# A hybrid streaming-encoder block on one core: x turned from token rows on TensorE, a plain first unit, and units, weights and gate writes in another order

## The chip, the core and the metric

The kernel runs on one core of a Trainium2 chip. A core has five engines with their own instruction queues: TensorE (PE, matrix products and transposes; its weight loads are shown apart as PEld), VectorE (DVE), ScalarE (ACT), GpSimd (POOL) and SyncE (SP, which here only issues DMAs). Sixteen DMA engines move data between the chip's memory and the core. The metric is the device time of one execution in microseconds (us); less is better.

## The reference

One layer: x and mem are normed and projected, three token mixers run side by side, each is projected back and gated, their sum is projected and added to x, and a gated feed-forward follows. There are 1024 tokens, 1024 channels and 256 memory tokens.

```python
h = _rmsnorm(x, norm_mix_g[l])
z = h @ w_in[l]
(hq, hf, hi, hg, fq, fk, fv, ff, mq, gate_logits) = jnp.split(z, pts, axis=-1)
y_a = _hgrn2_mixer(hq, hf, hi, hg, lower_bounds[l], hgrn_norm_g[l])      # 4 heads x 128, chunks
y_b = _fox_mixer(fq, fk, fv, ff, fox_f_bias[l], fox_q_norm_g[l], fox_k_norm_g[l])  # 8 heads x 64
mem_kv = _rmsnorm(mem, norm_mem_g[l]) @ mem_kv_w[l]
y_c = _memory_mixer(mq, mem_kv, mem_q_norm_g[l], mem_k_norm_g[l])        # 4 heads x 128
gates = jax.nn.sigmoid(gate_logits).reshape(B, T, N_BRANCH, D_MODEL)
merged = gates[:, :, 0] * (y_a @ w_br_hgrn[l]) + gates[:, :, 1] * (y_b @ w_br_fox[l]) + ...
x = x + merged @ w_out[l]
h2 = _rmsnorm(x, norm_ffn_g[l])
x = x + _conv_glu_ffn(h2, ffn_w_up[l], ffn_conv_w[l], ffn_conv_b[l], ffn_w_down[l])
```

`ff` (8 columns) gives the logits of the forget factors of the attention: log-sigmoid of them, summed along the tokens, is the bias of the attention's logits.

## The kernel before

**Products.** An fp32 product is made of three fp32r products (`mm3`): each operand is split into a high part (`h`, a rounding cast on ScalarE, line 115) and a low part (`l`, a subtraction on VectorE, line 123), and h·h, h·l and l·h are summed in PSUM (lines 109 to 111). The input projection is done in units by a Strassen-Winograd scheme on a 2 x 2 split of x (channel halves c, token halves n): seven products of 48 instructions instead of eight. The operands on the side of x are seven *families*: B11, B21, B22 are blocks of the normed x, T1, T2, T3, T4 are differences of them. Each has a high and a low tile.

**Stages.** (1) *Opening*: memory keys and values (`kv_chunk`, eight weight pieces wkv), the square sums of x, which is loaded with channels on partitions (`xT`, tiles xk), its rstd (by products with `ones`, spread over the partitions by `spread`), the forget logits as plain fp32 products of wff and x (line 315), and the first families. (2) *Five token-major units* (`tm_unit`), whose products are 256 columns wide: hi (values of HGRN), mq (memory queries), fox queries and keys of pairs 0 and 1, of pairs 2 and 3, and fv. A unit's outputs are normed per head (`head_norm`), turned by transposes and written to DRAM (kqd, vhd, hid, mqd). The steps of the memory attention (`mem_attn`) are queued in a list and woven into the units, up to STAGE_STEPS = 3 behind each product. (3) *Eighteen channel-major units* (`cm_unit`), 512 columns wide: six for HGRN (f, q, g), twelve for the gates, and then the branch projections. They are a generator, `fill`, that is woven as TensorE's filling work into (4) *the forgetting attention* (`fox_attn`, 8 heads; its steps have a higher priority by AHEAD = 300, and FOX_FILL says how many steps of fill go beside each head) and (5) *the HGRN mix* (`hgrn_mix`, 4 heads, HGRN_FILL steps beside each). The rest of the fill runs behind it, then (6) the *channel mixer* with `w_out`, `w_up`, `w_dn`.

**Order.** Instructions go to an engine's queue in the order that a scheduler gives at build time; each engine runs its queue in order. A DMA belongs to the queue of the engine that issues it, and stands there with its waits. A tile has a fixed number of buffers (`bufs`): whoever writes it next waits until its readers are done. A pool (`xp`, `rp`, `mp`, `ur`, `pfam`) holds space on a side of the on-chip memory until its release; the pool behind it starts where its space comes free.

**Names.** pp, lg, tr and po are the four kinds of PSUM banks. `w_tm` and `w_cm` are the weights of the two kinds of units, loaded into `raw` and `ur`; `ur` has 3 buffers of 512 KB here. `mskf` is the causal mask, `nf` the forget bias of a head, kh/qa/kl its keys and queries. uo is an output of a channel-major unit, written to `gd` (gates) or `hgd` (HGRN) and loaded from there later.

## Time and profile before

| | before |
|---|---|
| median of 3 runs | 1781.06 us (1780.62 to 1783.25) |
| profiled execution | 1782.18 us |
| its span | 1780.4 us |
| mean granted clock of TensorE | 0.982 |
| busy, share of the span | PE 96%, PEld 81%, DVE 70%, ACT 47%, POOL 27% |
| DMA | 272 MB, mean 153 GB/s |
| instructions in the profile | 25032 |

The profile counts an instruction as busy from its start to its end; since TensorE overlaps neighbours, its busy time is not its work, and the distance from start to start is the better price. `PEclk` is the TensorE clock that was granted, as a part of full speed. The table of stages gives the busy time of each engine in a stretch of the span with the number of its instructions in brackets. A row of a wait reads: who waited, for which engine's tile and line, total us, number, longest. A row in order of time reads: start, duration, engine, line, operation, out<-in, shape, count, and in brackets the idle time before it and who ended it.

### The profile page before, as it was taken

The numbers are of one execution on the slowest core, as the hardware profiler recorded it, in microseconds if no ns is written. First come the engines' busy times: TensorE is split into PE (matmuls) and PEld (weight loads), VectorE is DVE, ScalarE is ACT, GpSimd is POOL, SyncE is SP. The second block draws the span as 40 slices with busy tenths as digits, with TensorE's granted clock in tenths as the row PEclk, the third lists the DMA queues.
The fourth block names the chain that finished last, engine by engine and source line by source line (L and its number), as shares of the span: only waits on it lengthen the run. The fifth ranks groups of instructions, "written<-read, shape, count | busy, mean of one in ns | idle before, by whom it ended". The sixth has DMA issues, their size and how long they took to land.

```text
span 1780.4 us, 25032 instructions
## 1 busy us (share of the span) xinstructions
PE 1709.9 (96%) x8960; PEld 1443.3 (81%) x8960; DVE 1249.2 (70%) x2239; ACT 838.9 (47%) x1430; POOL 482.6 (27%) x496
## 2 busy tenths in 40 slices
PE   7799999989999999998999899999999999999999
PEld 5589999868888888877888788788888888878887
DVE  6967665447766676599799665787877877775654
ACT  6455555436565656566443333543433444433332
POOL 1644554335544434254223000111111111100000
PEclk9899999999999999999999999999999999999999
DMA  7034352484544443424543452455545444394772
GB/s 289 25 120 160 131 188 86 148 220 135 144 143 137 138 143 97 168 89 164 168 140 121 136 184 83 142 158 178 154 132 160 125 124 135 135 379 146 231 276 84
DMA packets 114398, 272.03 MB, mean 153 GB/s; under 512 B 11960, under 2 KB 29112, under 8 KB 113632
## 3 DMA queue, kind: packets, MB, share of 16 engines
q1 hardware_dynamic: 97088, 215.36, 36.8%
q0 software_dynamic: 14880, 52.96, 10.6%
q10 hardware_dynamic: 2304, 2.10, 0.3%
q8 instruction: 71, 1.16, 0.3%
q14 instruction: 55, 0.45, 0.1%
HBM read 202.93 MB, written 90.51 MB: 165 GB/s over the span
## 4 chain that ended last, share of the span: by engine, by line
PE 80%; DMA 6%; DVE 5%; issue 3%; POOL 3%; ACT 2%; SPq 0%; DVEq 0%; ACTq 0%; POOLq 0%
PE pp L109 17%; PE pp L111 17%; PE pp L110 17%; PE lg L111 4%; PE lg L109 4%; PE lg L110 4%; PE tr L109 2%; PE tr L110 2%; PE tr L111 2%; PE lg L1023 1%; DMA kh<-kqd 1%; POOL ws L424 1%; PE po L932 1%; PE lg L890 1%; PE lg L891 1%
## 5 line engine op out<-in xcount | busy, mean ns | idle before, releaser
L1282 POOL DMA_DIRECT2D rw<-in_w_up x44 | 24.3, 557 | 343.7 <-DVE wl L123 176.7
L115 ACT CAST wh<-s 128x512 fp32r<-128x512 f32 x85 | 51.9, 619 | 125.8 <-PE pp L110 65.3
L115 ACT CAST dwh<-wr 128x1024 fp32r<-128x1024 f32 (+1 forms) x42 | 41.1, 980 | 123.2 <-PE tr L110 42.0
L109 PE MATMUL pp<-yh,bwh 128*128 128x512 f32 x192 | 78.1, 412 | 5.1 <-ACT bwh L115 1.8
L115 ACT CAST wh<-rw 128x512 fp32r<-128x512 f32 x65 | 40.0, 619 | 86.1 <-PE pp L110 46.9
L1004 POOL TENSOR_TENSOR X<-X,kt 128x256 f32<-128x256 f32 x48 | 50.1, 1049 | 107.4 <-ACT X L1003 96.3
L110 PE MATMUL pp<-yl,bwh 128*128 128x512 f32 x192 | 78.1, 407 | 0.3 <-DVE yl L123 0.3
L111 PE MATMUL pp<-yh,bwl 128*128 128x512 f32 x192 | 77.8, 407 | 0.0
L123 DVE TENSOR_TENSOR dwl<-wr,dwh 128x1024 fp32r<-128x1024 f32 (+1 forms) x42 | 47.5, 1132 | 40.8 <-ACT dwh L115 40.4
L906 ACT ACTIVATE pt<-pt,st 128x128 f32<-128x128 f32 (+3 forms) x64 | 49.8, 778 | 51.0 <-DVE st L905 25.0
L123 DVE TENSOR_TENSOR ul<-us,uh 128x512 fp32r<-128x512 f32 x72 | 54.7, 763 | 25.7 <-ACT uh L115 24.8
L908 POOL TENSOR_SCALAR pt<-pt,st 128x128 f32<-128x128 f32 (+3 forms) x64 | 52.3, 819 | 61.0 <-DVE st L907 49.3
L677 POOL TENSOR_TENSOR us<-ur 128x512 f32<-128x512 f32 x36 | 51.8, 1438 | 56.6 <-DMA ur<-in_w_cm 40.0
L115 ACT CAST uh<-us 128x512 fp32r<-128x512 f32 x72 | 44.1, 617 | 36.7 <-PE pp L110 21.6
L123 DVE TENSOR_TENSOR wl<-s,wh 128x512 fp32r<-128x512 f32 x85 | 58.0, 682 | 4.9 <-ACT wh L115 4.9
L885 POOL TENSOR_TENSOR nfm<-nf,mskf 128x128 f32<-128x128 f32 x64 | 33.5, 523 | 91.6 <-DVE st L896 50.4
L123 DVE TENSOR_TENSOR wl<-rw,wh 128x512 fp32r<-128x512 f32 x65 | 43.7, 685 | 19.0 <-PE pp L111 15.1
L896 DVE CUSTOM_DVE_ANT_0 pt<-lg,nf 128x512 f32<-128x512 f32 (+2 forms) x80 | 41.3, 525 | 21.9 <-PE lg L891 11.1
L677 POOL TENSOR_TENSOR us<-us,ur 128x512 f32<-128x512 f32 x36 | 46.9, 1303 | 27.8 <-DVE ul L123 25.1
L110 PE MATMUL pp<-dbl,dwh 128*128 128x512 f32 x132 | 51.8, 392 | 1.5 <-DVE dbl L123 1.5
L123 DVE TENSOR_TENSOR pl<-tr,ph 128x512 fp32r<-128x512 f32 (+1 forms) x80 | 49.4, 629 | 4.5 <-ACT ph L115 4.2
L111 PE MATMUL pp<-dbh,dwl 128*128 128x512 f32 x132 | 51.9, 393 | 0.0
(580 smaller groups left out, 6312.0 us busy)
## 6 DMA issues: line engine op xcount, KB each, us to landing
rw<-in_w_up POOLq DMA_DIRECT2D x44, 512.0 KB, 4.7
ur<-in_w_cm SPq DMA_DIRECT2D x36, 512.0 KB, 3.7
sd<-in_w_dn POOLq DMA_DIRECT2D x30, 512.0 KB, 5.9
br<-yd SPq DMA_DIRECT2D x30, 512.0 KB, 5.0
gd<-uo SPq DMA_DIRECT2D x48, 256.0 KB, 2.1
gt<-gd SPq DMA_DIRECT2D x48, 256.0 KB, 3.0
yd<-fc SPq DMA_DIRECT2D x44, 256.0 KB, 2.2
raw<-in_w_tm SPq DMA_DIRECT2D x20, 512.0 KB, 5.5
```

What stands on the lines that cost most here:

```text
L109: PE.matmul(ps, lh, rh, start=first, stop=False, skip_group_check=more)
L110: PE.matmul(ps, lh, rl, start=False, stop=False, skip_group_check=more)
L111: PE.matmul(ps, ll, rh, start=False, stop=last, skip_group_check=more)
L115: S.copy(out, in_)
L123: return (sub or V).tensor_sub(l, src, h.bitcast(F32))
L677: G.tensor_add(t, a, b)
L885: G.tensor_tensor(nfm, nf[:, tsl], mskf, ALU.add)
L896: V.tensor_tensor_reduce(out=pt[:, s0 + lo:s0 + hi], in0=ps[:, lo:hi], in1=bias, op0=ALU.add, op1=ALU.max, scale=1.0, scalar=-3e38, accum_ ...
L906: S.activation(pt[:, :ns], pt[:, :ns], AF.Exp, bias=st[:, 2:3], accum_out=st[:, 3:4])
L908: G.tensor_scalar(pt[:, :ns], pt[:, :ns], st[:, 3:4], 0.0, ALU.mult, ALU.add)
L1004: G.tensor_mul(Xk, Xk, Kv[:, :, 0, :])
L1282: late["raw"] = G.dma_start(raw[:, 2 * i:2 * i + 2, :], src[:, 2 * i:2 * i + 2, :])
```

## The change

**x.** In the mixer, x comes no longer with channels on partitions but as eight tiles of 128 token rows (`x_rows`), placed in the space of the families T2 and T1, which are made later. ScalarE squares a row tile and sums along it in the same instruction (`row_square`); VectorE scales each row by its rstd (`row_norm`); TensorE turns the rows into the channel layout by 64 transposes (`turn_x`, four to a block of 128 x 512), and ScalarE copies each block out of PSUM with the channel's gain into a quarter `xq`. The square sums by products with `ones`, the spreading of rstd and `normed` are gone from the opening. `xT` is still loaded for the residual in the channel mixer.

**Units.** The first token-major unit is now mq, and it is a plain product (`first_unit`): eight products of 48 instructions with the families B11, B21, B12 (in T4's space) and B22. The other families are made beside it (`second_half`, `differences`, `third`, `last`), with subtractions on VectorE where GpSimd had them. The order of units is mq, hi, fox pairs 0 and 1, fv, fox pairs 2 and 3. All steps of the memory attention are queued in unit hi, two behind each product; the memory's keys and values are finished in the first unit and written by SP.

**Forget logits.** They are computed in unit two from the families B11, B21, B22 and T3, with weights split into a high and a low part that stand side by side in 40 columns: 16 products of 40 x 512 and 16 of 8 x 512 in fp32r.

**Others.** The first weight pieces of unit one and the x rows are loaded between the kv pieces. `head_norm` squares into the PSUM bank instead of a tile. A channel-major unit loads four pieces of 256 KB into 5 buffers. The 48 gate writes are issued by ScalarE instead of SP. HGRN_FILL is 32, 30, 28, 22 instead of 24, 24, 24, 20. The attention, the HGRN mix and the channel mixer keep their instructions; line numbers move by 15 to 50.

```diff
-HGRN_FILL = [24, 24, 24, 20]
+HGRN_FILL = [32, 30, 28, 22]
-STAGE_STEPS = 3
+STAGE_STEPS = 2
...
+    xr = [fam_tile(f, p, (P, 2, T), F32) for f in ("T2", "T1") for p in "hl"]
...
+    xq = [[xp.tile([P, 4, HB], F32, tag=f"x{c}{n}", name=f"x{c}{n}") for n in range(2)] for c in range(2)]
...
-        if q > 1:
-            load_x(q - 2)
-    SP.dma_start(ones, mats[:, P:2 * P])
+        load_x(q - 1)
+    SP.dma_start(ident, mats[:, 0:P])
+    load_x(3)
+    load_kv(4)
+    load_kv(5)
+    load_x(4)
+    tm_load(0, (0,))
+    load_x(5)
+    load_kv(6)
+    load_x(6)
+    tm_load(0, (1,))
+    load_x(7)
+    load_kv(7)
+    tm_load(0, (2, 3))
...
-    def forget_logits():
-        for k in range(KC):
-            for n in range(2):
-                PE.matmul(pairs[1][n][:8, :], wff[:, k, :], xk[k][:, n * HB:(n + 1) * HB], start=k == 0, stop=k == KC - 1)
...
+    def row_square(tb):
+        S.activation(ws_tile("sq"), x_row(tb), AF.Square, accum_out=rowsum[:, tb:tb + 1])
+
+    def row_norm(n):
+        ns = slice(4 * n, 4 * n + 4)
+        rstd_small(rt[:, ns], rowsum[:, ns], D)
+        for tb in range(4 * n, 4 * n + 4):
+            V.tensor_scalar(x_row(tb), x_row(tb), rt[:, tb:tb + 1], None, ALU.mult)
+
+    def quarter(c, n, k):
+        return xq[c][n][:, k, :]
+
+    def turn_x(c, n, k):
+        ps = ps_tr()
+        for b in range(4):
+            PE.transpose(ps[:, b * P:(b + 1) * P], x_row(4 * n + b)[:, (4 * c + k) * P:(4 * c + k + 1) * P], ident)
+        S.activation(quarter(c, n, k), ps, AF.Copy, scale=col(C_GX + 4 * c + k))
...
-    with tc.issue_after(spreads.ins):
-        forget_logits()
...
-    def normed(c, n, k, eng=V):
-        q = quarter(c, n, k)
-        if eng is V:
-            V.scalar_tensor_tensor(out=q, in0=q, scalar=col(C_GX + k + 4 * c), in1=rx[:, n * HB:(n + 1) * HB],
-                                   op0=ALU.mult, op1=ALU.mult)
-        else:
-            S.activation(q, q, AF.Copy, scale=col(C_GX + k + 4 * c))
-            G.tensor_mul(q, q, rx[:, n * HB:(n + 1) * HB])
-        return q
...
+    def first_half(c):
+        for k in range(4):
+            turn_x(c, 0, k)
+            family_block("B21" if c else "B11", k, quarter(c, 0, k))
+
+    for q in range(8):
+        if q < 4:
+            mem_chunk(2 * q)
+            mem_chunk(2 * q + 1)
+        kv_chunk(q)
+        if 0 < q < 4:
+            row_square(q - 1)
+        elif q == 4:
+            row_square(3)
+            row_norm(0)
+            for m in range(2):
+                S.copy(mkt[:, m, :], pairs[0][m])
+        elif q == 5:
+            first_half(0)
+            row_square(4)
+            row_square(5)
+        elif q == 6:
+            first_half(1)
+            row_square(6)
+    row_square(7)
+    row_norm(1)
...
+    def second_half():
+        fam["B12"] = [fam_tile("T4", p) for p in "hl"]
+        new_family("B22")
+        for c, name in enumerate(("B12", "B22")):
+            for k in range(4):
+                turn_x(c, 1, k)
+                family_block(name, k, quarter(c, 1, k))
+
+    def differences():
+        new_family("T2")
+        for k in range(4):
+            t2 = xp.tile([P, HB], F32, tag="tt", name="tt", bufs=2)
+            V.tensor_sub(quarter(0, 0, k), quarter(0, 0, k), quarter(0, 1, k))
+            V.scalar_tensor_tensor(out=t2, in0=quarter(0, 0, k), scalar=-1.0, in1=quarter(1, 1, k),
+                                   op0=ALU.mult, op1=ALU.subtract)
+            family_block("T2", k, t2)
+            V.scalar_tensor_tensor(out=quarter(1, 0, k), in0=t2, scalar=-1.0, in1=quarter(1, 0, k),
+                                   op0=ALU.mult, op1=ALU.subtract)
+        new_family("T1")
+        for k in range(4):
+            family_block("T1", k, quarter(0, 0, k))
...
+    def third():
         for k in range(4):
             q = quarter(0, 1, k)
-            G.tensor_sub(q, quarter(1, 1, k), q)
+            V.tensor_sub(q, quarter(1, 1, k), q)
             family_block("T3", k, q)
-        for k in range(4):
-            family_block("B22", k, quarter(1, 1, k), G)
...
+    def first_unit(put):
+
+        banks = [pairs[i] for i in (0, 1, 2, 0)]
+        ops = [tm_operand(raws[0, i]) for i in range(3)]
+        h, l = ws_tile("w4h", F32R), ws_tile("w4l", F32R)
+        split(S, h, l, raws[0, 3])
+        ops.append([t.rearrange("p (k c) -> p k c", k=4) for t in (h, l)])
+        for i, (c, n) in enumerate(((0, 0), (1, 0), (0, 1), (1, 1))):
+            for j, name in enumerate(("B12", "B22") if n else ("B11", "B21")):
+                tm_product(banks[i], ops[2 * c + j], name, j == 0)
+                if j:
+                    put(c, n, tm_out(0, banks[i], None), banks[i])
+                if i == 3:
+                    tm_load(1, range(2 * j, 2 * j + 2))
+                yield
...
+    def forget_logits():
+        wf = mem["mp"].tile([P, 2, KC, 40], F32R, tag="wf", name="wf")
+        wff, sm = (mem["mp"].tile([P, KC, 8], F32, tag=t, name=t) for t in ("wff", "sm"))
+        SP.dma_start(wff, w_ff)
+        V.memset(wf.bitcast(F32), 0.0)
+        V.tensor_add(sm[:, 0:4, :], wff[:, 0:4, :], wff[:, 4:8, :])
+        V.tensor_scalar(sm[:, 4:8, :], wff[:, 0:4, :], -1.0, None, ALU.mult)
+        for n, w in enumerate((wff, sm)):
+            split(S, wf[:, n, :, 0:8], wf[:, n, :, 32:40], w)
+        ff = ko_tile("ff", F32).rearrange("p a b -> p (a b)")
+        for n, names in enumerate((("B11", "B21"), ("B22", "T3"))):
+            ps = ps_tr()
+            sl = slice(n * HB, (n + 1) * HB)
+            for c, name in enumerate(names):
+                h, l = fam[name]
+                for k in range(4):
+                    w = wf[:, n, 4 * c + k, :]
+                    PE.matmul(ps[:40, :], w, h[:, k, :], start=c + k == 0, stop=False, skip_group_check=True)
+                    PE.matmul(ps[:8, :], w[:, 0:8], l[:, k, :], start=False, stop=c * k == 3, skip_group_check=True)
+            S.copy(ff[:8, sl], ps[32:40, :])
+            V.tensor_add(ff[:8, sl], ff[:8, sl], ps[:8, :])
+        SP.dma_start(ffd, ff[:8, :])
...
-            sq = mp.tile([P, HB], F32, tag="fsq", name="fsq").rearrange("p (c d) -> p c d", c=2 * nh)
+            sq = bank[b].rearrange("p (c d) -> p c d", c=2 * nh)
...
+    stage(0, put_mq, (None, second_half, memory, differences, None, third))
+    small_consts()
+    stage(1, put_hi, (last, mem_steps, forget_logits, forget_row))
     stage(2, put_fqk(0))
-    stage(3, put_fqk(1))
+    stage(3, put_fv)
...
+    stage(4, put_fqk(1))
...
-            SP.dma_start(gd[i, n], t)
+            S.dma_start(gd[i, n], t)
...
-        for i in range(2):
-            t = ur.tile([P, 2, HB], F32, tag="ur", name="ur", bufs=3)
+        for i in range(4):
+            t = ur.tile([P, HB], F32, tag="ur", name="ur", bufs=5)
             SP.dma_start(t, w_cm[u, i])
-            raw += [t[:, 0, :], t[:, 1, :]]
```

On TensorE, before the change, the end of the opening: the last forget products (L315, with wff the forget weights), eight products that spread rstd (L301, `ident` as an operand), and the first products of unit hi with family B11.

```order
L315 MATMUL pp<-xk_113,wff 8x512
L315 MATMUL po<-xk_113,wff 8x512
L315 MATMUL pp<-xk_114,wff 8x512
L315 MATMUL po<-xk_114,wff 8x512
L301 MATMUL tr<-ident,B22h 128x128 x8
L109 MATMUL pp<-wh,B11h 128x256
L110 MATMUL pp<-wl,B11h 128x256
L111 MATMUL pp<-wh,B11l 128x256
```

TensorE at the same place after the change; the x rows stand in the space named T1h and T1l, L337 is `turn_x`, and T4h and T4l are the memory tokens' space, as before.

```order
L109 MATMUL lg<-wh,T4h 128x512
L110 MATMUL lg<-wl,T4h 128x512
L111 MATMUL lg<-wh,T4l 128x512
L337 MATMUL tr<-ident,T1h 128x128 x2
L337 MATMUL tr<-ident,T1l 128x128 x2
L110 MATMUL pp<-wl,B11h 128x256
L111 MATMUL pp<-wh,B11l 128x256
L109 MATMUL pp<-wh,B11h 128x256
```

The products of the memory's values (out lg) now stand right ahead of the last turns and of unit one, and no forget products and no spreading stand between.

On SP, before the change, the start of the channel-major units and of the attention: the last writes of fv (vhd), the first weight loads (ur, 512 KB each), the writes of HGRN's inputs (hgd), and the first loads of head 0 (kh).

```order
L642 DMA vhd_74<-vo 128x1024
L735 DMA ur<-in_w_cm 128x1024
L722 DMA hgd_78<-uo 128x512
L642 DMA vhd_75<-vo 128x1024
L735 DMA ur<-in_w_cm 128x1024
L865 DMA kh_3572<-kqd_70 64x1024
L866 DMA kh_3572<-kqd_70 64x1024
```

SP at the same place after the change, with the writes of the last fox unit (kqd) where those of fv stood.

```order
L622 DMA kqd_72<-ko 256x1x512 x2
L784 DMA ur<-in_w_cm 128x512 x3
L622 DMA kqd_73<-ko 256x1x512 x2
L771 DMA hgd_78<-uo 128x512
L914 DMA kh_3661<-kqd_70 64x1024
L915 DMA kh_3661<-kqd_70 64x1024
```

The loads of head 0 now follow the first hgd write directly, behind smaller weight loads; the mask is issued behind 15 loads of the first two heads in both orders.

On TensorE, before the change, the end of the HGRN mix: state products (L1056, L1054), the transposes of the last output (L1075), and the branch products of the fill (yh, yl and bwh, bwl).

```order
L111 MATMUL pp<-yh_9620,bwl 128x512
L1056 MATMUL po<-St,qe 128x128
L1054 MATMUL po<-hi_9452,A 128x128
L1056 MATMUL po<-St,qe 128x128
L1075 MATMUL tr<-ident,o_9744 128x128 x4
L109 MATMUL pp<-yh_9622,bwh 128x512 x3
L110 MATMUL pp<-yl_9623,bwh 128x512
```

TensorE there after the change, first the last state products (L1105, L1103) and then the first transposes (L1124); 24 products of the fill stand between the two pieces.

```order
L1105 MATMUL po<-St,qe 128x128
L1103 MATMUL po<-hi_10026,A 128x128
L1105 MATMUL po<-St,qe 128x128
L110 MATMUL pp<-yl_9540,bwh 128x512
L111 MATMUL pp<-yh_9539,bwl 128x512
```

```order
L109 MATMUL pp<-yh_9539,bwh 128x512
L1124 MATMUL tr<-ident,o_10284 128x128
L110 MATMUL pp<-yl_9540,bwh 128x512
L111 MATMUL pp<-yh_9539,bwl 128x512
L109 MATMUL pp<-yh_9541,bwh 128x512
L1124 MATMUL tr<-ident,o_10284 128x128 x3
```

Products of the fill now stand ahead of the last transposes and between them.

More of the change, by code (lines that the diff above doesn't have):

```diff
@@ L342, in tile_block @@
-    for n in range(2):
-        spreads = spread(rx, rt, (n,))
-    with tc.issue_after(spreads.ins):
-        forget_logits()
-    def quarter(c, n, k):
-        return xk[k + 4 * c][:, n * HB:(n + 1) * HB]
     def new_family(name):
```

243 lines of the change are left out of this document (98 added, 145 removed).

## The prediction

> **What bounds the kernel now.** I read the table of stages first: for each stretch the busy time of every engine, the granted clock of TensorE and the share and rate of the DMA engines. The stretches are the opening up to the first product of a token-major unit, that unit, the other four units, the start of the forgetting attention, its body, the HGRN mix, its tail, the rest of the fill, and the channel mixer.
>
> ```profile
> core 0: us, PE busy (x) PEld busy (x) DVE busy (x) ACT busy (x) POOL busy (x), PEclk, DMA share, GB/s
> 0.00:57.50 57.50, 46.32 (x168) 27.12 (x169) 40.12 (x67) 33.59 (x48) 12.03 (x14) 0.97 0.61 223
> 57.50:119.50 62.00, 48.58 (x339) 46.81 (x338) 52.33 (x52) 31.22 (x51) 44.80 (x26) 0.83 0.29 95
> 119.50:331.70 212.20, 204.32 (x1698) 202.59 (x1696) 129.62 (x205) 108.69 (x215) 88.29 (x72) 0.98 0.37 127
> 331.70:400.00 68.30, 59.63 (x251) 47.65 (x252) 31.76 (x63) 28.75 (x55) 29.00 (x25) 0.95 0.74 222
> 400.00:745.00 345.00, 342.56 (x1832) 291.08 (x1831) 228.01 (x667) 202.80 (x413) 153.59 (x176) 1.00 0.44 132
> 745.00:1005.00 260.00, 243.38 (x1364) 205.77 (x1362) 221.84 (x432) 124.43 (x220) 89.43 (x81) 0.97 0.44 142
> 1005.00:1010.00 5.00, 3.83 (x9) 3.06 (x10) 4.26 (x8) 3.67 (x7) 0.00 (x0) 0.50 0.00 0
> 1137.00:1780.40 643.40, 634.32 (x2743) 514.17 (x2741) 459.24 (x625) 252.38 (x349) 62.17 (x101) 1.00 0.55 173
> ```
>
> TensorE sets the pace nearly everywhere, and a change can win only by taking work from it or by closing its holes. From 400 to 745 us and in the channel mixer it is 99% busy, so those stages are fixed by its instructions. The unit from 57.5 to 119.5 us is the odd one: busy 48.6 of 62 us at a clock of 0.83. Busy time overlaps in a pipelined engine, so I price TensorE by the pitch from start to start, read from the order of time:
>
> ```profile
> 13.20 0.40 PE L110 MATMUL pp<-wl,T4h 128*128 128x512 f32 x1
> 13.44 0.40 PE L111 MATMUL pp<-wh,T4l 128*128 128x512 f32 x1
> 42.84 1.02 PE L315 MATMUL pp<-xk,wff 128*8 128x512 f32 x2
> 43.70 1.02 PE L315 MATMUL po<-xk,wff 128*8 128x512 f32 x2
> 168.22 0.60 PE L624 MATMUL tr<-ident,mpt 128*128 128x128 f32 x4
> 168.57 0.36 PE L109 MATMUL lg<-wh,B11h 128*128 128x256 f32 x1
> 328.30 0.28 PE L110 MATMUL po<-wl,T4h 128*128 128x256 f32 x1
> 329.14 0.28 PE L111 MATMUL po<-wh,T4l 128*128 128x256 f32 x1
> 64.27 0.41 PE L110 MATMUL pp<-wl,B11h 128*128 128x256 f32 x1
> 64.48 0.41 PE L109 MATMUL pp<-wh,B11h 128*128 128x256 f32 x1
> ```
>
> A 512-column fp32r product takes 0.235 us, a forget-logit product in fp32 0.86 (43.70 - 42.84), a transpose 0.09 (0.35 for four), and a 256-column product 0.12 (0.84 for seven intervals; I use 0.119). At the halved clock of 64 us the last costs 0.21. By these prices unit one, 7 x 48 = 336 products, is 40 us of work in 62: **22 us are lost**. The four later units, 1536 products and 160 transposes, are 197 us in 212: 15 lost. The waits of TensorE in unit one say why:
>
> ```profile
> PE pp L111 <- DVE B11l L123: 6.7, 2, 5.0
> PE pp L111 <- DVE T2l L123: 4.1, 1, 4.1
> ```
>
> It waits for the low parts of the families that VectorE cuts from x; the half clock follows those holes. VectorE is slow there (52 of 62 us) because GpSimd works 45 us beside it:
>
> ```profile
> L123 DVE TENSOR_TENSOR T2l<-T4h,T2h 128x512 fp32r<-128x512 f32 x4 | 4.9, 1217 | 0.0
> L123 DVE TENSOR_TENSOR B21l<-xk,B21h 128x512 fp32r<-128x512 f32 x4 | 2.6, 674 | 0.0
> ```
>
> The same subtraction takes 1.22 us in one case and 0.67 in the other.
>
> **The change part by part.** *Opening.* Removed from TensorE: 16 forget products (13.7 us), the ones and spread products (about 3.8). Added: 64 turns of x (5.8), 48 products for the plain unit (8 x 48 instead of 7 x 48: 5.7), and 32 fp32r forget products (7.5). The work hardly changes, 17.5 out and 19 in; what changes is where it stands. Half of the turns go between the kv products, which wait for weights anyway. The plain unit needs only four families, straight from the turned x, instead of seven made of sums, and 16 GpSimd operations on x are gone, so I price VectorE's subtractions at 0.67.
>
> When can unit one start? The loads run at full rate:
>
> ```profile
> 0.00:20.00 20.00, 13.55 (x47) 9.98 (x48) 11.48 (x27) 13.18 (x21) 0.30 (x5) 1.00 0.90 314
> 20.00:40.00 20.00, 15.27 (x65) 10.98 (x64) 16.02 (x25) 14.83 (x19) 2.38 (x3) 0.93 0.85 328
> 28.70 1.04 ACT L115 CAST wh<-wkv 128x1024 fp32r<-128x1024 f32 x1 [0.74 <-DMA wkv<-in_w_mkv]
> 33.65 1.03 ACT L115 CAST wh<-wkv 128x1024 fp32r<-128x1024 f32 x1
> ```
>
> On SP's queue the seventh kv piece now has 1.5 MB more ahead of it (the memory rows and the first unit weight) and the eighth 1.0 MB more, which at 0.32 MB/us is 4.7 and 3.1 us: the seventh lands near 33.5 instead of 28.7, the eighth near 36. Two ScalarE casts (1.04 each), two subtractions, the last kv products and a turn put the unbroken run of unit-one products at **42 us**. From that row to the first channel-major product the new order holds 1918 products, 180 transposes and 32 forget products: 228 + 16 + 7.5 = 252 us. To it I add lost time: for the later four units the 15 of before without the 2.7 named below, 12.4; for unit one 8. The 8 is a choice between 0 and the 22 of before, nearer the low end as VectorE's rows up to the first query transposes (some 30 at 0.67) end about when TensorE comes to them, so a hole of a few us is likely, not many. 42 + 252 + 20.4 = 314.4 against 331.8: **-17.4**, with 0 and 22 for unit one from -25 to -3. The tensor_scalar on a whole x row has no row here: below by half the 1.22 of a 1024-wide tensor operation, above by it, 8 of them; hidden under the kv wait, and the 5 us between these ends are in the range. The forget products now stand in unit two, between products of that unit, so nothing hides them: their 7.5 us are counted in full.
>
> *Start of the channel-major units and of the attention.*
>
> ```profile
> 327.31 1.29 SPq L735 DMA_DIRECT2D ur<-in_w_cm  x3
> 331.84 0.50 PE L109 MATMUL pp<-B11h,uh 128*128 128x512 f32 x1 [2.42 <-ACT uh L115]
> 364.20 0.51 SPq L865 DMA_DIRECT2D kh<-kqd  x1
> 382.03 0.34 SPq L859 DMA_DIRECT2D mskf<-in_mats  x1
> 390.30 0.45 POOL L885 TENSOR_TENSOR nfm<-nf,mskf 128x128 f32<-128x128 f32 x1 [13.15 <-DMA mskf<-in_mats]
> 391.15 0.69 PE L890 MATMUL lg<-kh,qa 128*128 128x384 f32 x1 [6.07 <-DVE st L896]
> ```
>
> The first weights came late because the memory attention held their space to the end of unit five; it now ends 96 products earlier, so the 2.7 us hole closes (it is in the -17.4). The mask is queued behind 15 loads of the first two heads and lands 26 us after the first of them. In the new order that first load follows one hgd write, some 9 us after the units begin, so the mask lands near 35 us after them; TensorE reaches the product that needs it after 128 products, near 31. The hole shrinks from 6.1 to 4-5 us and the half clock behind it stays: **-2**, between -8 (no hole, no half clock) and +5 (a hole as long as the wait for all loads).
>
> *HGRN and fill.* The fill table grows from 92 to 112 steps, but the order shows 698 fill products under the HGRN chain for 673, so no more than 25 x 0.23 = 6 us move. The tail is different:
>
> ```profile
> 999.88 0.39 PE L1056 MATMUL po<-St,qe 128*128 128x128 f32 x2
> 1003.42 1.25 PE L1075 MATMUL tr<-ident,o 128*128 128x128 f32 x4 [3.16 <-ACT o L1072]
> 1006.17 1.65 PE L109 MATMUL pp<-yh,bwh 128*128 128x512 f32 x3 [1.50 <-ACT yh L115]
> ```
>
> Before, the last output transposes follow the last state product at once and TensorE stands 3.2 and 1.5 us, and the 5 us from 1005 run at a clock of 0.50, 2.5 lost: 7.2 in all. In the new order 24 products (5.5 us) stand between, and fill remains behind: -7.2 if all goes, 0 if another wait comes; I take **-7**, since the 5.5 us of cover exceed the longer of the two holes.
>
> *Gate writes.* 48 writes leave SP for ScalarE, which pays their issue and holds everything behind them:
>
> ```profile
> L633 ACTq DMA_DIRECT2D yd<-yo x16: 326/326/348, 169.3 to 327.8; - x16
> SPq L703 <- ACT uo L702: 27.2, 8, 9.5
> ```
>
> 48 x 0.326 = 15.6 us on an engine that is 59% busy in the attention and 48% in HGRN: hidden by its idle time, **+1** where it feeds the HGRN chain (0 to +16). SP's 27 us of waits for those outputs go, but no load behind them bounded TensorE, so I count nothing. The finer weight loads and the new unit order cost nothing that I can place; the channel mixer keeps its instructions: 0.
>
> Sum: -17.4 - 2 - 7 + 1 = -25.4. The profiled execution took 1782.18 us (span 1780.4 and 1.8 around it), 1.1 above the median of the runs: 1782.2 - 25.4 = **1757**.
>
> **The rivals.** *Unit one stays bound by VectorE and ScalarE* (20%): the four families, head norms and differences are as much for them as before, TensorE loses the 22 again. For it: both are near 85% full in that stretch by my count. Against: GpSimd is out of the way. 14 us back: 1771. *Turns leave the clock low* (10%): if TensorE runs at half clock from the turns at 28 us to past 42, the first 42 unit-one products cost 0.21 instead of 0.12 and the kv products as much: 5 us, 1762. The run of four at 168 us was at full clock, but inside a stream of products; no row shows turns alone. [...] *ScalarE blocks* (12%), the slower side: 30 of the 48 gate writes in the new order also wait for an earlier DMA's slot, which may stand on SP's queue. If each holds ScalarE for the median 2.1 us of a gate write, that is 63 us; it decides once such holds exceed ScalarE's idle time between two HGRN steps, and with half on the path it is +31: 1788. *That the fill table does nothing* is in the forecast already.
>
> **How the numbers follow.** Forecast 58%, 1757 (own range 1745 to 1768); rivals 20%, 10%, 12% at 1771, 1762, 1788. The range 1742 to 1780 takes in the unknowns of the opening (-25 to -3) and of the tail, and leaves out the blocked ScalarE and the far ends. A measurement of this kernel can tell about 0.2%, 3.6 us, from no change. Faster: nearly all of the forecast (56), 16 of the second case, 10 of the third, 82%; same 6%; slower 12%.
>
> **What would show it.** Right: the first channel-major product near 314 us, unit-one products unbroken from 42, a clock of 1.0 there, subtractions at 0.67, no 3.2 us hole at the last output transposes. Wrong: TensorE waiting for families or for e after 42 us, ScalarE idle at gate writes, a new hole where the branches begin near 820 us, or the mask hole grown.

## The result, and the profile after

| | before | after |
|---|---|---|
| median (range) of 4 runs each | 1780.84 us (1778.28 to 1783.25) | 1757.72 us (1756.36 to 1758.42) |
| ratio to before, 95% interval | | 0.9869 (0.9852 to 0.9887) |
| profiled execution, its span | 1782.18, 1780.4 us | 1758.42, 1756.6 us |

The change makes the kernel 23 us faster; 1757 was forecast. The stages of the kernel after, in the columns of the prediction's table: a stretch of the opening, the opening up to the unbroken run of unit-one products, unit one, the other four units, the start of the attention, the HGRN mix, its tail, and the channel mixer from the same product on as before.

```profile
20.00:40.00 20.00, 15.26 (x72) 10.93 (x71) 13.20 (x20) 19.39 (x36) 2.75 (x3) 0.91 0.73 288
0.00:45.40 45.40, 33.47 (x142) 24.50 (x143) 27.63 (x51) 38.32 (x65) 3.08 (x9) 0.96 0.76 283
45.40:103.00 57.60, 52.50 (x430) 52.30 (x429) 40.91 (x67) 36.40 (x66) 7.23 (x4) 0.94 0.26 91
103.00:316.46 213.46, 207.74 (x1706) 202.41 (x1704) 131.75 (x204) 113.81 (x220) 91.86 (x75) 0.98 0.41 140
316.46:384.00 67.54, 63.42 (x295) 52.40 (x295) 36.46 (x96) 31.80 (x63) 33.20 (x31) 0.95 0.66 195
709.00:960.00 251.00, 239.05 (x1346) 203.62 (x1345) 217.26 (x419) 123.81 (x222) 95.39 (x83) 0.97 0.42 141
960.00:1010.00 50.00, 50.00 (x227) 41.42 (x226) 44.41 (x68) 21.33 (x35) 1.01 (x1) 1.00 0.58 198
1109.90:1756.60 646.70, 637.90 (x2742) 514.26 (x2740) 459.20 (x625) 251.74 (x349) 61.92 (x101) 1.00 0.54 172
```

Unit one now holds 430 TensorE records in 57.6 us where it held 339 in 62, and GpSimd works 7 us there instead of 45. The tail of the HGRN mix, which stood and ran at half clock before, is full: 50.00 of 50 us. But the channel mixer takes longer: 643.4 us before from 1137.00, 646.7 now.

TensorE in order of time, at the places that the prediction named: the first unbroken unit-one products behind a turn, the new wait in unit one, the end of unit five with the first channel-major product, the mask's product, the last state products and the first transposes of the last HGRN output, and the first product of the channel mixer that waits for its weights (that last row of before behind it).

```profile
45.27 0.38 PE L337 MATMUL tr<-ident,T1l 128*128 128x128 f32 x2
45.41 0.36 PE L110 MATMUL pp<-wl,B11h 128*128 128x256 f32 x1
45.61 0.28 PE L111 MATMUL pp<-wh,B11l 128*128 128x256 f32 x1
45.73 0.28 PE L109 MATMUL pp<-wh,B11h 128*128 128x256 f32 x1
...
76.31 0.58 PE L109 MATMUL pp<-wh,T4h 128*128 128x256 f32 x1 [5.10 <-DVE ko L123]
...
313.36 1.97 PE L606 MATMUL pp<-ident,e 128*128 128x128 f32 x8 [2.27 <-DVE e L601]
316.46 0.80 PE L109 MATMUL pp<-B11h,uh 128*128 128x512 f32 x1 [1.14 <-DVE ko L612]
...
353.54 0.45 PE L939 MATMUL lg<-kh,qa 128*128 128x384 f32 x1 [3.81 <-DVE st L945]
...
960.60 0.39 PE L1105 MATMUL po<-St,qe 128*128 128x128 f32 x2
...
966.31 0.27 PE L1124 MATMUL tr<-ident,o 128*128 128x128 f32 x1
...
1112.86 0.50 PE L109 MATMUL pp<-T3h,wh 128*128 128x512 f32 x1 [2.55 <-ACT wh L115]
```

```profile
1140.15 0.79 PE L109 MATMUL pp<-T3h,wh 128*128 128x512 f32 x1 [2.54 <-ACT wh L115]
```

So the gain is 15.4 us by the first channel-major product (331.84 to 316.46), 27.3 us by the channel mixer (1140.15 to 1112.86), and 23.8 us at the end of the span: **3.5 us are given back in the channel mixer, whose instructions are the same.** The median of all runs hides how large the first part was. The 15.4 us are of one pair of profiles: in runs 3 and 5 below, whose opening and units are those of before, the first channel-major product stands at 329.26 and 329.10 us, and in runs 1, 2 and 4, which have those of the change, at 317.63, 317.43 and 316.38. Over these profiles the first part is worth 11.5 to 15.5 us.

### The profile page after: what moved, and what is told of

It reads as the page before. It is cut to its first block, busy times and chain, and to the rows that moved or that the text cites. A ratio compares the mean times of both kernels' runs of the same rounds, so it can differ in the third digit from the quotient of the medians.

```text
span 1756.6 us, 25190 instructions
## 1 busy us (share of the span) xinstructions
PE 1706.7 (97%) x9040; PEld 1447.6 (82%) x9040; DVE 1228.1 (70%) x2230; ACT 848.2 (48%) x1463; POOL 440.6 (25%) x471
## 4 chain that ended last, share of the span: by engine, by line
PE 83%; DMA 5%; DVE 4%; ACT 3%; POOL 2%; issue 1%; SPq 1%; ACTq 0%; DVEq 0%; POOLq 0%
PE pp L109 17%; PE pp L110 17%; PE pp L111 17%; PE lg L109 4%; PE lg L110 4%; PE lg L111 4%; PE tr L109 2%; PE tr L110 2%; PE tr L111 2%; PE lg L1072 1%; PE po L981 1%; DMA gd<-uo 1%; PE lg L939 1%; DMA nf<-negFd 1%; PE lg L940 1%
## 5 line engine op out<-in xcount | busy, mean ns | idle before, releaser
L726 POOL TENSOR_TENSOR us<-ur 128x512 f32<-128x512 f32 x36 | 46.7, 1297 | 44.9 <-DMA ur<-in_w_cm 27.6
L123 DVE TENSOR_TENSOR ul<-ur,uh 128x512 fp32r<-128x512 f32 x54 | 48.3, 896 | 7.8 <-ACT uh L115 6.8
L726 POOL TENSOR_TENSOR us<-us,ur 128x512 f32<-128x512 f32 x36 | 47.6, 1324 | 24.0 <-DVE ul L123 11.5
```

The lines of the kernel that those rows point to most:

```text
L123: return (sub or V).tensor_sub(l, src, h.bitcast(F32))
L726: G.tensor_add(t, a, b)
```

## The experiments

Twelve kernels ran, each beside the kernel before on the same chip; a ratio is to that kernel before.

**1. Gate writes on SyncE again.**

```diff
-            S.dma_start(gd[i, n], t)
+            SP.dma_start(gd[i, n], t)
```

> The changed kernel with one edit: the 48 gate writes are issued by SyncE again. Theory (the forecast's term of +1 us): the issue of 48 x 0.33 us is hidden by ScalarE's idle time, so the time stays within 0.2% of the changed kernel, 1755 to 1759 us. Rival A (ScalarE blocks behind gate writes and this eats part of the gain): 5 us or more faster, at or under 1752, and holes of TensorE that end at ScalarE shrink. Rival B (the move took SyncE's waits for outputs away from the weight loads behind them): slower, 1762 or more, with new waits of GpSimd or TensorE for ur loads.

Measured: 1756.87 us (1751.71 to 1762.87), ratio 0.987 (0.9841 to 0.9898). The same as the change. In the change's trace, ScalarE's gate writes and the waits for an earlier transfer that stand before 30 of them (duration min/median/max in ns):

```profile
L752 ACTq DMA_DIRECT2D gd<-uo x48: 326/326/362, 489.6 to 826.1; - x48
L752 ACTq EVENT_SEMAPHORE  x30: 17/17/17, 489.1 to 826.0; - x30
```

Each of the 30 waits lasted 17 ns, where other waits on ScalarE's queue in this trace (line 115) last up to 5.27 us: the transfer was always done. The rival of a blocked ScalarE had its condition in the program and no price on the chip.

**2 and 3. The fill table alone.** The changed kernel with the old table, and the kernel before with the new one.

```diff
-HGRN_FILL = [32, 30, 28, 22]
+HGRN_FILL = [24, 24, 24, 20]
```

> The changed kernel with the old fill table of the HGRN mix (24, 24, 24, 20). Theory (the forecast's -7 at the tail is due to the larger table): the last output transposes again follow the last state product at once, TensorE stands some 3 and 1.5 us there and runs at half clock after, 1763 to 1766 us. Rival (the earlier units shifted the fill, the table does little): no hole over 1 us at the last output transposes, 1756 to 1759 us.

> The kernel before with only the new fill table (32, 30, 28, 22). Theory (table alone closes the tail hole): no wait of 3.2 us at the last output transposes, 1772 to 1776 us. Rival (the table needs the rest of the change, or moves the hole to where the fill passes from units to branches): 1779 to 1783 us, with a hole of the same size elsewhere.

Measured: 1757.32 us (1753.07 to 1758.63), ratio 0.9867 (0.9847 to 0.9887), and 1780.81 us (1778.01 to 1784.06), ratio 0.9999 (0.9987 to 1.0011). The rivals hold in both. With the old table the changed kernel has no wait of TensorE from 955 to 985 us; with the new table the kernel before keeps both of its holes, in order of time:

```profile
1001.07 1.25 PE L1075 MATMUL tr<-ident,o 128*128 128x128 f32 x4 [3.16 <-ACT o L1072]
1003.81 1.65 PE L109 MATMUL pp<-yh,bwh 128*128 128x512 f32 x3 [1.49 <-ACT yh L115]
```

The table is not what closed the tail. Nor did it bring more fill under the HGRN chain: between the first and the last product of the chain stand 673 products of the fill in the profile before, 671 after the change and 673 in run 2 (a few records can be missing). Products stand between the last state product and the first of the transposes behind it in every version of the changed kernel: 24 in the change, 24 with the gate writes back on SyncE (run 1), 22 with the old table (run 2), 24 with unit one by seven products (run 8) and 45 with the unit fv last (run 11). So none of these four does it alone. What is left is the rest of the change, the turned x, the finer weight loads and the order of the other units among it; which part shifts the fill against the HGRN chain was not tried on the chip.

**4. The mask's load first.**

```diff
-    SP.dma_start(mskf, mats[:, 2 * P:3 * P])
+    with tc.high_priority(2 * AHEAD):
+        SP.dma_start(mskf, mats[:, 2 * P:3 * P])
```

> The changed kernel with the load of the causal mask ahead of the 15 loads of the first two heads on SyncE, nothing else. Theory (the hole of 3.8 us at 349.7 us and the half clock behind it come from the mask standing last in that queue): the hole is gone, 1751 to 1754 us. Rival (the loads of head 0 themselves are the limit: the forget bias nf or the keys land as late): a hole of 2 us or more stays at the same product and the time is 1756 to 1759 us.

Measured: 1758.09 us (1756.6 to 1759.02), ratio 0.9873 (0.9854 to 0.9891). Neither theory. GpSimd's first use of the mask comes at 341.03 us instead of 352.70, and no product of the attention waits near 350 us any more. But TensorE waits elsewhere, in order of time:

```profile
354.90 0.79 PE L109 MATMUL pp<-T3h,uh 128*128 128x512 f32 x1 [3.25 <-ACT ue L731]
...
833.33 3.65 PE L1073 MATMUL lg<-X 128*128 128x64 f32 x16 [5.56 <-DVE A L1069]
```

A channel-major product waits for the copy of its bank (ue) in place of the mask, and at 833 us, where the fill passes from units to branches, the HGRN chain has a wait of 5.56 us, longer than any there in the change. The mask was the last wait there, not the only one.

**5 and 6. Where the left tiles lie.** The channel mixer's loss called for a cause that is in none of its instructions. In the programs as built, the constants' pool is 704 bytes smaller after the change (`ones` has one column, wff is gone from it), so every tile on the left side of the on-chip memory, the operands dbh and dbl of the down projection among them, begins elsewhere: at an offset of 384 modulo 512 bytes of a partition before and 192 after. One unused tile moves them by 64 bytes.

```diff
     mhalf = cp.tile([P, 16], F32, tag="mhalf", name="mhalf")
+    pad = cp.tile([P, 16], F32, tag="pad", name="pad")
+    nc.gpsimd.memset(pad, 0.0)
```

> The kernel before with an unused 64-byte tile in the constants' pool, so that the tiles on the left side of the on-chip memory begin 64 bytes later (offset 448 in place of 384, modulo 512); every product stays. What is asked: the channel mixer's products stand 230.0 ns apart in the down projection before the change and 231.8 after it, in all runs so far, though its instructions are the same. Theory P (the place of the left tiles sets this pitch: the change moved them by 704 bytes): the pitch of the down projection changes by 1 ns or more in one direction and the channel mixer by 2 us or more. Rival (something else that the change brought, or the state of the chip): 230.0 ns and 738 us from the last branch product as before, 1780 to 1782 us.

> The changed kernel with the same unused 64-byte tile, so the left tiles begin at offset 256 in place of 192, modulo 512 (now a multiple of 128 bytes as before the change). Theory P: the pitch of the down projection returns to 230.0 ns, the channel mixer takes 3 to 4 us less, 1753 to 1755 us. Rival: 231.8 ns and the time of the changed kernel, 1756 to 1759 us.

Measured: the kernel before with the pad 1784.43 us (1781.19 to 1791.36), ratio 1.0024 (1.0007 to 1.0041), so a little slower; the changed kernel with it 1756.03 us (1755.53 to 1756.58), ratio 0.9862 (0.9837 to 0.9886). The last 801 products of the down projection, from the first of them to the start of the last, 800 distances. Each fence is one kernel, and the first number after the stretch is its length: before, after, before with pad, after with pad, and run 9 below.

```profile
1591.64:1775.63 183.99, 183.99 (x801) 150.10 (x800) 106.77 (x111) 62.13 (x68) 0.00 (x0) 1.00 0.59 195
```

```profile
1566.65:1752.12 185.47, 185.47 (x802) 150.28 (x800) 106.68 (x111) 62.09 (x68) 0.00 (x0) 1.00 0.56 191
```

```profile
1589.09:1774.56 185.47, 185.47 (x801) 150.16 (x800) 106.55 (x111) 62.12 (x68) 0.00 (x0) 1.00 0.57 191
```

```profile
1563.45:1750.11 186.66, 186.66 (x802) 150.16 (x800) 107.24 (x112) 62.10 (x68) 0.00 (x0) 1.00 0.57 192
```

```profile
1558.88:1742.87 183.99, 183.99 (x801) 150.21 (x800) 106.59 (x111) 62.12 (x68) 0.00 (x0) 1.00 0.58 195
```

Divided by 800, and beside it the mean distance from start to start of the up projection's 512-column products, over those below 260 ns in some 290 us of it:

| kernel | left tiles' offset, modulo 256 bytes | down projection, ns | up projection, ns |
|---|---|---|---|
| before | 128 | 230.0 | 231.7 |
| before + 64 bytes | 192 | 231.8 | 232.7 |
| after | 192 | 231.8 | 232.7 |
| after + 64 bytes | 0 | 233.3 | 231.9 |
| after - 64 bytes (run 9) | 128 | 230.0 | 231.7 |

The pad gives the kernel before the very pitch of the changed one, in both projections; theory P holds. Its second half missed: an offset of 0 is not like 128, the down projection gets slower still and the up projection faster. There the 256-column products of the token-major units change too, which the table does not show: 116.9 ns apart in this run (over the distances below 130 ns), 118.3 in the kernel before and 118.4 in the kernel after.

**7. The family cuts later, by program order.**

```diff
-    stage(0, put_mq, (None, second_half, memory, differences, None, third))
+    stage(0, put_mq, (None, second_half, memory, None, None, differences))
...
-    stage(1, put_hi, (last, mem_steps, forget_logits, forget_row))
+    stage(1, put_hi, (third, last, lambda: (mem_steps(), forget_logits()), forget_row))
```

> The changed kernel with the families T2 and T1 cut after the last product of unit one, T3 and T4 in unit two. Theory (TensorE stands 5.3 us at 70.9 us since the bank's reader, the low part of the memory queries on VectorE, is queued behind these cuts): the hole shrinks to under 2 us, the first channel-major product comes 3 to 5 us earlier (312 to 313.5 us), 1752 to 1755 us. Rival (the families are only due later): the wait comes back in unit two, ahead of the products with T2 or T1, and the first channel-major product stays near 316.5 us, 1756 to 1759 us.

Measured: 1759.55 us (1755.77 to 1761.12), ratio 0.9879 (0.9855 to 0.9903). A miss as an experiment: VectorE's queue in unit one had the same order as in the change, and the same wait stands there. The edit moved the subtractions in the program, and the scheduler left them where they stood in the queue.

```profile
77.12 0.58 PE L109 MATMUL pp<-wh,T4h 128*128 128x256 f32 x1 [5.10 <-DVE ko L123]
```

**8. Unit one by seven products again**, with x turned as in the change.

```diff
-        for i, _ in enumerate(tm_unit(u, put) if u else first_unit(put)):
+        for i, _ in enumerate(tm_unit(u, put)):
...
-    stage(0, put_mq, (None, second_half, memory, differences, None, third))
+    stage(0, put_mq, (second_half, differences, memory, third, None, last))
```

(B12 is not cut then, and `last` goes from unit two to unit one.)

> The changed kernel with unit one made of seven products with all seven families instead of eight plain ones with four. It saves 48 products, 5.7 us. Theory (unit one was bound by VectorE and ScalarE that cut the families; the plain unit takes them off its path): TensorE waits for T2, T1 or T3 in unit one, 10 us or more, the first channel-major product comes at 320 to 330 us, 1761 to 1772 us. Rival (the turned x alone did it): the first channel-major product at 311 to 314 us, 1752 to 1755 us.

Measured: 1767.82 us (1763.21 to 1771.51), ratio 0.9927 (0.99 to 0.9954). The theory holds. VectorE's cuts of T2 in that kernel (min/median/max ns), the waits of TensorE in unit one, and the first channel-major product:

```profile
L123 DVE TENSOR_TENSOR T2l<-tt,T2h x8: 676/682/692, 63.3 to 1110.9; 128x512 fp32r<-128x512 f32 x8
```

```profile
64.02 0.50 PE L111 MATMUL pp<-wh,T2l 128*128 128x256 f32 x2 [2.06 <-DVE T2l L123]
68.70 0.58 PE L109 MATMUL pp<-wh,T2h 128*128 128x256 f32 x1 [4.19 <-ACT T2h L115]
75.98 0.58 PE L111 MATMUL pp<-wh,T2l 128*128 128x256 f32 x1 [6.05 <-DVE T2l L123]
...
326.45 0.79 PE L109 MATMUL pp<-B11h,uh 128*128 128x512 f32 x1 [1.14 <-DVE ko L612]
```

It does 5.7 us less work and comes to the channel-major units 10.0 us later (326.45 for 316.46), with VectorE's subtraction at 0.68 us, where its mean in the kernel before was 1.22. So about two thirds of the 15.4 us gained up to there hang on the plain unit, which needs no T2; the rest of the change ahead of that point gives the other third. With the spread of that point from profile to profile, this share is rough.

**9. Left tiles at offset 128.**

```diff
-    hgc = cp.tile([P, 1], F32, tag="hgc", name="hgc")
-    fqs = cp.tile([P, 1], F32, tag="fqs", name="fqs")
-    mgk = cp.tile([P, 1], F32, tag="mgk", name="mgk")
+    gcs = cp.tile([P, 3], F32, tag="gcs", name="gcs")
+    hgc, fqs, mgk = (gcs[:, i:i + 1] for i in range(3))
```

> The changed kernel with three constant columns put into one tile, so that the left tiles begin 64 bytes earlier: offset 128 modulo 512 in place of 192, which is 128 modulo 256 as in the kernel before (384). Theory P (the place of the left tiles modulo 256 sets the pitch: 384 gave 230.0 ns in the down projection, 192 and 448 gave 231.85, 256 gave 233.3): 230.0 ns, the channel mixer at 738 to 739 us in place of 742, 1753 to 1755 us. Rival (only the distance between these very addresses counts): another pitch, 231 to 234 ns, and 1755 to 1759 us.

Measured: 1754.86 us (1749.12 to 1755.74), ratio 0.9846 (0.9814 to 0.9879), and the pitch of before to the nanosecond (table above). As theory P had it.

**10. The cuts of T2, T1 and T3 held behind the first query splits** on VectorE's and ScalarE's queues, so that the edit reaches them this time (`issue_after` sets the order in a queue, no wait).

```diff
-            split(S, h, l, ptr)
+            mem.setdefault("ko", []).append((S.copy(h, ptr), V.tensor_sub(l, ptr, h.bitcast(F32))))
             return
...
+        hold = ExitStack()
+        for i in mem["ko"][1]:
+            hold.enter_context(tc.issue_after(i.ins))
         for k in range(4):
```

> The changed kernel with the families T2, T1 and T3 held behind the first two query splits on VectorE's and ScalarE's queues (the edit of the run before, by program order, did not reach those queues). Theory (the 5.3 us hole at 70.9 us and the half clock behind it are the queue's order on VectorE): the hole is under 1.5 us, the first channel-major product 5 to 7 us earlier (310 to 312 us), 1751 to 1753 us. Rival (VectorE simply has too much work up to there): TensorE waits as long for a family or for head norms later in units one and two, first channel-major product at 315 us or later, 1756 to 1759 us.

Measured: 1754.71 us (1751.85 to 1759.15), ratio 0.9854 (0.9822 to 0.9887). Half of each theory: the wait of 5.10 us is gone, and none stands from 60 to 95 us, but unit two now begins with one for a low part of the queries:

```profile
97.73 0.39 PE L109 MATMUL pp<-wh,B11h 128*128 128x256 f32 x1 [1.62 <-DVE ko L617]
```

The first channel-major product comes at 314.09 us, 2.4 earlier and not 5 to 7 (the change and runs 1, 2 and 4 have it between 316.38 and 317.63). Between 80 and 120 us TensorE loses 5.3 us (distances beyond the usual one of their shape) where it lost 2.1 in the change, at this wait and around the transposes of normed outputs, so part of the hole is VectorE's amount of work and not its order.

**11. The unit fv last, as in the kernel before.**

```diff
-    stage(3, put_fv)
+    stage(3, put_fqk(1))
...
-    stage(4, put_fqk(1))
+    stage(4, put_fv)
```

> The changed kernel with the last two token-major units in the order of the kernel before: fox pairs 2 and 3, then fv. Theory (the hole of 2.3 and 1.1 us ahead of the first channel-major product and the half clock behind come from the head norms and transposes of a fox unit that stands last): the first channel-major product 3 to 5 us earlier (312 to 313.5 us), 1753 to 1756 us. Rival (the start of the attention then waits for what fv writes last): the hole near 350 us grows by as much, 1757 to 1762 us.

Measured: 1762.93 us (1758.97 to 1764.32), ratio 0.9895 (0.9857 to 0.9932). The rival. The wait ahead of the first channel-major product goes, and that product comes at 315.21 us, but from 320 to 360 us TensorE loses 10.7 us in place of 6.4, most of it at the start of the attention:

```profile
342.28 0.69 PE L939 MATMUL lg<-kh,qa 128*128 128x384 f32 x1 [4.32 <-DVE st L945]
```

**12. Runs 9 and 10 together.**

> The changed kernel with the two edits that helped: left tiles at offset 128 modulo 512, and the families T2, T1 and T3 held behind the first query splits. If the two savings add (4 to 5 us in the channel mixer, some 2.4 us ahead of the first channel-major product): first channel-major product at 313 to 315 us, 230.0 ns in the down projection, 1749 to 1752 us, ratio to the kernel before 0.982 to 0.985. If one takes the other back: 1754 us or more.

Measured: 1749.18 us (1746.77 to 1753.8, 5 runs), ratio 0.982 (0.9801 to 0.984), below the interval of the change (0.9852 to 0.9887). This version beats both kernels, and the savings add: its down projection has 230.0 ns, and its first channel-major product stands at 311.68 us, earlier than forecast.

## Why the prediction was right, and where its parts were not

The total was right (1757 for 1757.7), and not by each of its terms. That it is met to a microsecond is luck: terms that missed by 1 to 4 us cancel.

- **Opening and units, -17.4 forecast, -15.4 measured.** The mechanism was right, and run 8 shows it: the plain unit takes VectorE's cuts off TensorE's path. The one wait left in unit one (5.10 us), with the half clock behind it (0.50 from 74.09 to 80.92 us), costs 7.6 us (what the distances from start to start between 60 and 80 us exceed the usual one of their shape) for the 8 assumed. It is not for a family, though, but for a bank that VectorE reads late. Two steps failed. First, the unbroken run begins at 45.4 us and not at 42: I priced the loads, and they land as early as forecast or earlier (the seventh kv piece at 31.8 us for 33.5, the eighth at 35.7 for 36), but ScalarE, with squares, copies and casts, is 19.39 of 20 us busy from 20 to 40, and casts these pieces only at 35.56 and 39.91. Second, "the 2.7 us hole closes" was wrong: the weights do come in time, but the last unit is now one with head norms and transposes, and TensorE waits 2.27 and 1.14 us for these instead. Run 11 takes this wait away and pays more at the start of the attention.
- **VectorE at 0.67.** Right: 0.68 to 0.69 in the opening and unit one. The scaling of an x row, which had no row, takes 0.75 us, near the lower of its two ends. The 1.22 of before is a mean: the four cuts of T2 take 0.67, 0.67, 1.74 and 1.78 us. Both slow ones have GpSimd at work beside them, but so have the two of 0.67. So that GpSimd had slowed VectorE fits the traces and was the author's reading; no run tried it by itself, and run 8 shows that it was not the larger part.
- **Start of the attention, -2.** The hole went from 6.07 to 3.81 us, for "4-5" forecast, and the mask's product stands 37.1 us behind the first channel-major one, with the mask forecast at 35. Right. By the distances beyond the usual one of their shape, TensorE lost 12.0 us from 331.8 to 400 us before and 8.9 from 316.4 to 384 after.
- **Tail, -7.** Right in size: both holes (3.16 and 1.50) and the half clock are gone; by the same count TensorE lost 8.7 us from 995 to 1011 us before and 0.3 from 960 to 1011 after. The ground named for it, products standing between, is seen in the order; that the table brought them there is refuted by runs 2 and 3, and what did is open.
- **Gate writes, +1.** Within what run 1 can tell, nothing.
- **Channel mixer, 0.** This is the term that failed: +3.5 us. "The channel mixer keeps its instructions" is true and was no ground for 0. Of its 924 down products at 1.85 ns and some 1850 up products at 1.0 ns, 1.7 and 1.8 us are the tiles' place, shown by runs 5 and 9; some 1.5 us more are a half clock at the start of the down projection in this one execution (below), and about as much is saved at the start of the stage, where the kernel before ran at half clock from 1139.74 to 1143.15 us and the kernel after did not. So the place of the tiles is the whole of the 3.5 us, as near as these traces tell.

The attention and HGRN, from the first channel-major product to the channel mixer, brought 11.9 us (27.3 - 15.4) where -2, -7 and +1 make 8; that surplus of 3.9 balances the 3.5 of the channel mixer and hides the failed term. By the counts above it is for the most part the tail (8.4 instead of 7), the start of the attention (3.1 instead of 2) and the +1 of the gate writes, which did not come.

Of the rivals, unit one stays bound (1771) is near what run 8 measures without the plain unit, 1767.8. The blocked ScalarE is refuted by the 17 ns and by run 1. For the turns and the clock, the row at 45.41 answers: unit-one products right behind a turn stand 0.12 us apart, at full clock. Only ahead of that, behind eight turns with waits of 1.97, 0.44 and 0.28 us between them, does the clock halve (0.50), from 36.54 to 39.95 us; five products and four turns take 3.3 us there instead of the 1.5 of the prediction's prices:

```profile
34.64 0.44 PE L337 MATMUL tr<-ident,T2h 128*128 128x128 f32 x2 [1.97 <-ACT x L338]
...
36.67 1.22 PE L109 MATMUL lg<-wh,T4h 128*128 128x512 f32 x2 [0.28 <-ACT wh L115]
...
39.97 0.39 PE L111 MATMUL lg<-wh,T4l 128*128 128x512 f32 x1
```

In run 2 the same eight turns follow the same waits (1.96, 0.44 and 0.28 us), and the clock stays full (the last number but two of each row):

```profile
35.09:38.50 3.41, 2.04 (x10) 1.14 (x10) 2.44 (x5) 3.41 (x6) 0.70 (x1) 1.00 0.00 0
38.51:41.92 3.41, 3.18 (x18) 2.69 (x18) 1.62 (x3) 3.41 (x7) 0.00 (x0) 1.00 0.45 156
```

So the turns alone did not set the clock here, and no run shows a long stretch of turns alone; the last section shows what the clock went with.

## What to carry to other kernels

When an algorithm saves products by sums of operands, look who makes the sums: at the start of this kernel, with nothing else to do for TensorE, eight plain products (1757.72 us) beat seven that wait (1767.82). Closing one wait is worth only what the next one leaves: in run 4 a wait of 3.81 us went, one of 3.25 and one of 5.56 stood elsewhere, and the time was the same (1758.09 us). The order of a helper engine with a full queue had to be set in that queue (run 10: the wait of 5.10 us gone); by the program's order it stayed (run 7: 5.10 us still). And when a stage with the same instructions changes its time, compare where its tiles lie (230.0 and 231.8 ns a product here) and the clock that it was granted (1.00 and 0.50 over 3.41 us) before looking for anything else.

## What the runs showed of the hardware

**The pitch of the channel mixer's products went with the place of the left tiles.** Between the kernels of the table, a move of all left tiles by 64 bytes changed the mean distance of 512-column fp32r products by 0.8 to 1.8 ns (0.3 to 0.8%). In the down projection it was 230.0 ns at offsets 384 and 128 modulo 512 (before, run 9), 231.8 at 448 and 192 (run 5, after), and 233.3 at 256 (run 6). In the output projection no difference was seen: its products stand 226.8 ns apart before and 226.7 after. Over the 800 distances of the down projection, those before lie between 228 and 232 ns; after the change 89, every ninth, are 239 or 240, and the others 229 to 235. Which operand matters, and what makes the rhythm, stays open: all left tiles moved at once.

**The same wait was followed by half clock in some executions and not in others.** At the start of the down projection TensorE waits 1.53 us for the same subtraction in both kernels; after it, in order of time, first the kernel after, then before:

```profile
1537.38 0.50 PE L110 MATMUL pp<-dbl,dwh 128*128 128x512 f32 x1 [1.53 <-DVE dbl L123]
...
1538.84 0.63 PE L110 MATMUL pp<-dbl,dwh 128*128 128x512 f32 x1
1539.27 0.63 PE L111 MATMUL pp<-dbh,dwl 128*128 128x512 f32 x1
```

```profile
1564.14 0.50 PE L110 MATMUL pp<-dbl,dwh 128*128 128x512 f32 x1 [1.53 <-DVE dbl L123]
...
1565.18 0.40 PE L111 MATMUL pp<-dbh,dwl 128*128 128x512 f32 x1
1565.42 0.39 PE L110 MATMUL pp<-dbl,dwh 128*128 128x512 f32 x1
```

0.43 us apart in the one, 0.23 in the other. Runs 4, 5, 11 and 12 have the slow form too, runs 1 to 3 and 6 to 10 the fast one, so it follows neither the change nor the tiles' place. It costs some 1.5 us in the kernel after.

The granted clock shows what it went with. From 30 us on it changes 23 times in the profile before and 18 times in the one after, and each change lies a whole multiple of 3.41 us, to within 0.02 us, from the first (37.23 us before, 36.54 after). So where these points lie in the span differs between the two. Here is the stretch between two such points that holds the wait, with the stretch behind it, in the kernel after and in run 2 (length, then TensorE's busy time first; the clock is the last number but two):

```profile
1535.00:1538.41 3.41, 1.76 (x6) 1.16 (x7) 3.41 (x5) 0.82 (x1) 1.05 (x2) 1.00 0.94 267
1538.41:1541.82 3.41, 3.41 (x9) 2.64 (x8) 3.41 (x5) 0.00 (x0) 1.08 (x2) 0.50 1.02 401
```

```profile
1536.96:1540.37 3.41, 1.88 (x7) 1.25 (x8) 3.41 (x4) 0.37 (x1) 1.05 (x2) 1.00 0.96 281
1540.38:1543.78 3.40, 3.40 (x16) 2.71 (x16) 3.40 (x4) 0.00 (x0) 1.08 (x2) 1.00 1.02 403
```

TensorE is busy for 1.76 us of the stretch that holds the wait in the kernel after, and 0.50 follows; for 1.88 us in run 2, and 1.00 follows. In the kernel before, the wait lies from 1562.61 to 1564.14 us, on both sides of such a point, and the clock stays at 1.00:

```profile
1563.00:1566.42 3.42, 2.28 (x10) 1.88 (x11) 3.42 (x4) 0.00 (x0) 1.59 (x3) 1.00 0.93 321
1566.42:1569.83 3.41, 3.41 (x17) 2.77 (x16) 3.41 (x4) 0.00 (x0) 0.54 (x1) 1.00 1.03 414
```

In the profiles before and after together, from 30 us on, a stretch at full clock with less than 1.5 us of busy time was followed by half clock in 12 of 12 cases, one with 1.5 to 2.0 us in 6 of 10, and one with more in 2 of 962. So in these two profiles the half clock went with stretches in which TensorE did little, and whether one wait of 1.53 us made such a stretch differed with where it fell between the points. This is read from the traces alone; no run moved a wait on purpose.
